# A SwiGLU block by Strassen-like products: four pairs a half in w_down's long passes, loads queued as buffers come free, three residues a half by DMA, gate's activation one half step later

## Chip, cores, metric

One Trainium2 chip, one of its cores. The metric is device time in microseconds (us) of the kernel on that core; lower is better. Times come from runs of the whole kernel and, for the parts, from one profiled execution.

## What is computed

One layer over 256 tokens of width 2048, all in float32:

```python
h  = x + W_out [ DiffAttn(group A heads) ; ConformerConv(group B channels) ]( RMSNorm(x) )
y  = h + SwiGLU( RMSNorm(h) )

a  = hn @ w_gate                      # hn (256, 2048), w_gate and w_up (2048, 5632)
bu = hn @ w_up
y  = h + (silu(a) * bu) @ w_down      # w_down (5632, 2048)
```

The change lies in the last three lines (the SwiGLU part). What comes before them (the projection w_in, attention, convolution, w_out) fills the first 390 us of the profile and keeps its code.

## The kernel before

**Precision.** A float32 operand is split into a part rounded to the matmul's format (`hi`) and a residue (`lo = x - hi`), and a product is made of three matmuls: hi·hi, lo·hi and hi·lo. Activations are the stationary side, weights the moving side, 128 k-rows by 512 columns at a time. Of a weight tile, ScalarE casts `hi` and VectorE subtracts for `lo`. For some chunks ("by DMA", `by_dma` in `round_chunk`) ScalarE instead writes the rounded `-raw` to `lo` (L323) and a transfer issued from POOL, GpSimd's queue, adds `raw` to it (L324); VectorE is spared.

**Units of work.** The SwiGLU part is a list of chunks that TensorE multiplies one after the other. Two kinds stand in it:

- a *chunk of two* (`g` or `u`): two k-rows of one block of 512 columns, for both halves of the tokens. 12 matmuls (`multiply_two`, L1014, L1015, L1020). A `g` chunk belongs to the first of two column blocks, a `u` chunk to the second (w_gate and w_up in a gate/up block; columns n and n + 1 of w_down in a pass).
- a *pair* (`s`): two k-rows and both column blocks at once, by seven products of sums in place of eight (a 2x2 scheme in the manner of Strassen and Winograd). 21 matmuls (`multiply_pair`, L993 to L995) into seven PSUM banks. Its weights need sums first (`wt`, L966 to L968, VectorE), then two casts (`wh`, L969 and L972, ScalarE) and two residues (`wlb`, `wlt`, L975 and L976, VectorE). Its activations need the matching sums: `make_forms` for the normalized input, `make_down_forms` for SwiGLU's product.

**Blocks and passes.** The 5632 hidden columns are 11 blocks of 512, in groups of 4, 4 and 3 (`FGROUPS`). A group's gate/up blocks come first (four pairs, four `g` and four `u` chunks each, in the order `ORDER = "sggsggsuusuu"`; block 0 goes another way); then w_down's *pass* over that group's rows, in two *halves* of two column blocks each (`down_pass`). A pass of a group of four ("long pass") has 16 k-rows: `ND = 2` pairs from its first two blocks and 6 `g` and 6 `u` chunks of two a half, in the orders `DORDERS[4]`. After the last chunk that is no `u` ("half end"), `bank_sums` adds the banks up on VectorE (L1094 to L1099), and in a gate/up block ScalarE takes gate's activation (L1105); after the last chunk, VectorE adds the two `u` banks (L1113, or L1154 in a pass) and multiplies (L1115). The product is transposed on TensorE (`ps_a`, L831) and becomes `ahi`/`alo` of the pass (L840, L842), or, for the first `ND` rows of a group's first two blocks, `raw_act` (L834), from which `make_down_forms` makes the pairs' operands in the following blocks. A pass adds its results to `hd` in DRAM by transfers from POOL (L1138, L1155).

**What sets the order.** Each engine runs its own list, and waits between the lists are by semaphores. The lists are written by one loop, `run_chunks`: at step t it rounds the chunk three ahead (`HI_AHEAD`), splits two ahead, and multiplies chunk t. Everything else (sums, activations, transposes, forms) runs in generators that are resumed once or more for each chunk; `lag(n)` lets n resumptions pass. SyncE's list of loads is one queue in that order too: a load that waits for its buffer holds back those behind it. Raw tiles have 5 buffers, pairs' raw tiles (`wb`) 2.

## Time and profile before

| | |
|---|---|
| median of 3 runs (lowest to highest) | 1048.29 us (1047.63 to 1048.34) |
| profiled execution: its time, its span | 1048.92 us, 1047.1 us |
| mean granted TensorE clock | 1.000 |
| busy: TensorE, VectorE, ScalarE, POOL | 99%, 86%, 59%, 10% of the span |
| matmuls in the trace | 4663 |
| read from and written to HBM | 204.24 MB, 9.44 MB |
| SwiGLU part | from 391 us on; long passes at 517 to 602 us and 769 to 854 us |

In the profile's rows a line reads: line, engine, operation, output<-inputs, shapes, count | busy us, mean ns | idle time of the engine just before, and what ended it. PE is TensorE's matmuls, PEld its weight loads, DVE VectorE, ACT ScalarE, POOL GpSimd (only its queue matters here). A window's row has its borders and length, then each engine's busy time with its count of instructions, the granted clock, the share of the 16 DMA engines and GB/s. Line numbers are those of the kernel before.

### The profile page before, as it was taken

The page shows a single profiled execution, that of the slowest core. Times are in us where ns is not written, and L with a number is a line of the kernel's source. Part 1 is how long each engine was busy: PE and PEld are TensorE (multiplying, and loading weights), DVE is VectorE, ACT ScalarE, POOL GpSimd, SP SyncE. Part 2 cuts the span into 40 slices and gives each one's busy share as a digit, 9 for nine tenths or more (in the row PEclk, how much of TensorE's full clock was granted, in tenths as well). Part 3 has the DMA queues.
Part 4 walks back from the last instruction along what each step waited for, and adds up shares of the span by engine and source line. Part 5 has one row for each costly group of instructions (what it writes and reads, how often), then busy time and mean ns, then how long its engine had stood idle before and what let it go on. Part 6 is the DMA issues. An engine that isn't in the chain of part 4 may idle for free.

```text
span 1047.1 us, 12933 instructions
## 1 busy us (share of the span) xinstructions
PE 1036.2 (99%) x4663; PEld 852.5 (81%) x4663; DVE 900.6 (86%) x1095; ACT 621.6 (59%) x786; POOL 100.5 (10%) x143
## 2 busy tenths in 40 slices
PE   9999999999999999999999999999999999999998
PEld 7888887877788788888888888888888888888886
DVE  7899889898765599999787898999878789989897
ACT  7544666755756565776463657666644446657442
POOL 0130122201100100000001010000000110000010
PEclk9999999999999999999999999999999999999999
DMA  9657654453546566987867789879757879798683
GB/s 335 227 182 280 212 163 167 154 181 134 177 153 226 194 223 214 268 266 236 232 210 188 217 271 273 256 217 285 248 175 241 219 208 291 222 287 267 187 265 85
DMA packets 113936, 231.30 MB, mean 221 GB/s; under 512 B 7504, under 2 KB 8656, under 8 KB 113616
## 3 DMA queue, kind: packets, MB, share of 16 engines
q1 hardware_dynamic: 104864, 203.71, 56.9%
q0 software_dynamic: 8864, 26.74, 13.4%
q8 instruction: 36, 0.59, 0.2%
q14 instruction: 28, 0.23, 0.1%
q10 hardware_dynamic: 144, 0.03, 0.0%
HBM read 204.24 MB, written 9.44 MB: 204 GB/s over the span
## 4 chain that ended last, share of the span: by engine, by line
PE 61%; DMA 2%; DVE 2%; issue 1%; ACT 0%; DVEq 0%; POOLq 0%
PE q L1020 12%; PE q L1014 12%; PE q L1015 12%; PE q L995 8%; PE q L993 7%; PE q L994 7%; DMA raw<-in_w_down_dram 1%; PE ps_a L831 1%; DMA wlo<-raw 1%; PE acc L365 1%; PE acc L359 1%; PE acc L360 1%; DVE wlo L329 1%; DVE wlt L976 0%; DVE wt L966 0%
## 5 line engine op out<-in xcount | busy, mean ns | idle before, releaser
L320 ACT CAST whi<-raw 128x1024 fp32r<-128x1024 f32 (+1 forms) x273 | 281.5, 1048 | 141.6 <-PE acc L360 58.9
L329 DVE TENSOR_TENSOR wlo<-raw,whi 128x1024 fp32r<-128x1024 f32 (+1 forms) x239 | 287.8, 1218 | 73.5 <-ACT whi L320 73.3
L972 ACT CAST wh<-wt 128x2048 fp32r<-128x2048 f32 x52 | 99.6, 1914 | 77.6 <-DVE wt L968 76.9
L976 DVE TENSOR_TENSOR wlt<-wt,wh 128x2048 fp32r<-128x2048 f32 x52 | 119.1, 2290 | 14.9 <-ACT wh L972 14.7
L359 PE MATMUL acc<-whi,xhi 128*128 128x512 f32 x320 | 126.9, 397 | 1.0 <-ACT whi L320 0.9
L360 PE MATMUL acc<-whi,xlo 128*128 128x512 f32 x320 | 125.2, 391 | 0.0
L1014 PE MATMUL q<-whi,chi 128*128 128x512 f32 x320 | 125.2, 391 | 0.0
L1015 PE MATMUL q<-whi,clo 128*128 128x512 f32 x320 | 124.5, 389 | 0.0
L993 PE MATMUL q<-wh,fhi 128*128 128x512 f32 x280 | 109.9, 393 | 0.0
L994 PE MATMUL q<-wh,flo 128*128 128x512 f32 x280 | 109.1, 390 | 0.0
L517 DVE SCALAR_TENSOR_TENSOR y<-upad,cw,y 128x256 f32<-128x256 f32 x240 | 102.2, 482 | 2.2 <-ACT y L510 2.2
L1014 PE MATMUL q<-whi,ahi 128*128 128x512 f32 x256 | 100.2, 391 | 0.0
L1015 PE MATMUL q<-whi,alo 128*128 128x512 f32 x256 | 99.6, 389 | 0.0
L975 DVE TENSOR_TENSOR wlb<-wb,wh 128x1536 fp32r<-128x1536 f32 x52 | 91.1, 1752 | 1.8 <-ACT wh L969 1.8
L365 PE MATMUL acc<-wlo,xhi 128*128 128x512 f32 x320 | 87.8, 396 | 2.0 <-DVE wlo L329 2.0
L1020 PE MATMUL q<-wlo,chi 128*128 128x512 f32 x320 | 85.7, 390 | 0.2 <-DMA wlo<-raw 0.2
L969 ACT CAST wh<-wb 128x1536 fp32r<-128x1536 f32 x52 | 76.6, 1474 | 0.0
L365 PEld LDWEIGHTS acc<-wlo,xhi 128*128 128x128 f32 x320 | 59.7, 189 | 15.3 <-DVE wlo L329 3.3
L359 PEld LDWEIGHTS acc<-whi,xhi 128*128 128x128 f32 x320 | 60.4, 189 | 14.3 <-ACT whi L320 1.9
L1020 PEld LDWEIGHTS q<-wlo,chi 128*128 128x128 f32 x320 | 59.9, 188 | 13.2 <-DMA wlo<-raw 0.8
L360 PEld LDWEIGHTS acc<-whi,xlo 128*128 128x128 f32 x320 | 60.4, 189 | 12.2
L1014 PEld LDWEIGHTS q<-whi,chi 128*128 128x128 f32 x320 | 60.1, 188 | 12.3
(230 smaller groups left out, 1739.1 us busy)
## 6 DMA issues: line engine op xcount, KB each, us to landing
raw<-in_w_in_dram SPq DMA_DIRECT2D x79, 512.0 KB, 4.6
raw<-in_w_down_dram SPq DMA_DIRECT2D x64, 512.0 KB, 7.2
raw<-in_w_gate_dram SPq DMA_DIRECT2D x48, 512.0 KB, 7.5
raw<-in_w_up_dram SPq DMA_DIRECT2D x48, 512.0 KB, 6.2
wb<-in_w_up_dram SPq DMA_DIRECT2D x40, 512.0 KB, 3.7
wb<-in_w_gate_dram SPq DMA_DIRECT2D x40, 512.0 KB, 4.9
wlo<-raw POOLq DMA_DIRECT2D x34, 512.0 KB, 7.1
raw<-in_w_out_dram SPq DMA_DIRECT2D x32, 512.0 KB, 4.2
```

The lines of the kernel that those rows point to most:

```text
L320: act.copy(c["hi"], c["raw"])
L329: dve.tensor_tensor(c["lo"], c["raw"], c["hi"].bitcast(F32), ALU.subtract)
L359: pe.matmul(ps[m], xhi[:, ms], hi[:, j, :], start=c["first"] and j == 0, stop=False)
L360: pe.matmul(ps[m], xlo[:, ms], hi[:, j, :], start=False, stop=False)
L365: pe.matmul(ps[m], xhi[:, ms], lo[:, j, :], start=False, stop=c["last"] and j == nk - 1)
L517: dve.scalar_tensor_tensor(y[:, ct, :], src, wk, y[:, ct, :], ALU.mult, ALU.add)
L976: dve.tensor_tensor(lot, c["t"], c["hi"][:, :SUMMED].bitcast(F32), ALU.subtract)
L993: pe.matmul(ps, hi, c["hi"][:, w], start=bool(first), stop=False)
L994: pe.matmul(ps, lo, c["hi"][:, w], start=False, stop=False)
L1014: pe.matmul(ps, xs[i][0][:, ms], hi[:, i, :], start=i == 0 and bool(c["first"].get(qs[m])), stop=False)
L1015: pe.matmul(ps, xs[i][1][:, ms], hi[:, i, :], start=False, stop=False)
L1020: pe.matmul(sum_bank(c, qs[m]), xs[i][0][:, ms], lo[:, i, :], start=False, stop=i == 1 and bool(c["last"].get(qs[m])))
```

## The change

Long passes get four pairs a half (`NDS = (4, 4, 2)`) in the order of the gate/up blocks, so 4 `g` and 4 `u` chunks are left; three of those eight get their residue by DMA. The activation's forms become twice as long and are spread over other buffers (`dhs`, `dls`). The last block's transposes use the same PSUM pool as the others' (`closing`). Loads are queued when, by the order of the loop, the buffer that they wait for has been split, raw tiles and pairs in the order in which their buffers come free (`load_freed`), no longer pairs by a fixed lead. Gate's activation is put one resumption later (`SILU_LAG`), and the additions to `hd` up to three (`HD_LAG`). The short last pass keeps two pairs and its orders.

```diff
@@ -86,8 +86,10 @@
 HD = N // P
-ND = 2
-DORDERS = {4: ("gguuggsguugsuu", "sgggugggusuuuu"), 3: ("gguusggsuu", "gggsgsuuuu")}
+NDS = (4, 4, 2)
+DORDERS = {4: (ORDER, ORDER), 3: ("gguusggsuu", "gggsgsuuuu")}
+HD_LAG = 3
+DOWN_BY_DMA = {4: (dict(g=(0, 1), u=(1,)),) * 2, 3: (dict(g=(), u=()),) * 2}
@@ -96,7 +98,9 @@
-PAIR_AHEAD = 6
+PAIR_BUFS = 2
+SILU_LAG = 1
@@ -386,32 +390,60 @@
         n = len(chunks)
-        i = j = p = 0
-        behind = [k for k in range(n) if chunks[k].get("kind") == "s"][NS]
+        i = j = 0
+        pairs = [k for k in range(n) if chunks[k].get("kind") == "s"]
+        raws = [k for k in range(n) if chunks[k].get("kind") != "s" and not chunks[k].get("spare_raw")]
+        loaded, split = set(), set()
+        def load(k):
+            if k not in loaded:
+                loaded.add(k)
+                if k in before:
+                    before[k]()
+                chunks[k]["load" if chunks[k].get("kind") != "s" else "fetch"](chunks[k])
+        def split_next():
+            chunks[j]["split"](chunks[j])
+            split.add(j)
+        ahead = [[k for k in which if k >= pairs[2]] for which in (raws, pairs)]
+        place = [{k: a for a, k in enumerate(which)} for which in (raws, pairs)]
+        def freed(side, t):
+            which, bufs = ((raws, RAW_BUFS), (pairs, PAIR_BUFS))[side]
+            if not ahead[side] or pairs[2] - 1 not in loaded:
+                return None
+            k = which[place[side][ahead[side][0]] - bufs]
+            return k if k in split and (t >= k or not chunks[k]["by_dma"]) else None
+        def load_freed(t):
+            while True:
+                ready = [(k, side) for side in range(2) if (k := freed(side, t)) is not None]
+                if not ready:
+                    return
+                load(ahead[min(ready)[1]].pop(0))
...
             while j < min(i, t + 1 + lo_lead):
-                chunks[j]["split"](chunks[j])
+                split_next()
                 j += 1
-            while p < min(n, t + 1 + PAIR_AHEAD):
-                if chunks[p].get("kind") == "s":
-                    if p < behind and p > t + hi_lead:
-                        break
-                    load_pair(chunks[p])
-                p += 1
+            load_freed(t)
             while i < min(n, t + 1 + hi_lead):
-                if i in before:
-                    before[i]()
-                chunks[i]["load"](chunks[i])
+                load(i)
+                for which in ahead:
+                    if i in which:
+                        which.remove(i)
                 chunks[i]["round"](chunks[i])
...
                 if hi_lead == lo_lead:
-                    chunks[j]["split"](chunks[j])
+                    split_next()
                     j += 1
             while j < min(n, t + 1 + lo_lead):
-                chunks[j]["split"](chunks[j])
+                split_next()
                 j += 1
+            load_freed(t)
             chunks[t]["multiply"](chunks[t])
@@ -819,7 +851,7 @@
     def transposed(j, aa):
-        last = j + 1 in FIRSTS
+        last = j + 1 in FIRSTS and NDS[group_of(j)[0]] < HD
         b = j - group_of(j)[1]
@@ -829,12 +861,15 @@
                     pe.transpose(pt[:, i, m * P : (m + 1) * P], aa[m][:, c : c + P], ident)
-            if b < 2 and 2 * t < ND:
-                raw_act[b] = lhs.tile([P, 2, S], F32, tag=("lhi", "llo")[b], name=f"ar{j}")
-                act.copy(raw_act[b], pt)
+            g = group_of(j)[0]
+            nd = NDS[g]
+            if b < 2 and 2 * t < nd:
+                if not b and not t:
+                    raw_act[g] = ffn["pool"].tile([P, 2, nd, S], F32, tag="draw", name="raw_act")
+                act.copy(raw_act[g][:, b, 2 * t : 2 * t + 2, :], pt)
                 yield from lag(3 if last else 6)
-                if b:
-                    start(make_down_forms(group_of(j)[0]))
+                if b and 2 * t + 2 == nd:
+                    start(make_down_forms(g))
                 continue
@@ -842,7 +877,10 @@
                 actT[j * (N // P) + 2 * t + i] = (hi[:, i, :], lo[:, i, :])
-            yield from lag(1 if last else 4)
+            yield from lag(1 if last else 3 if closing(j) else 4)
+    def closing(j):
+        return j + 1 in FIRSTS and NDS[group_of(j)[0]] == HD
@@ -857,39 +895,46 @@
-        fp = ffn["pool"]
+        nd = NDS[g]
         gap = lambda: lag(5 if FGROUPS[g] == 4 else 2)
-        a11, a21 = (raw_act[0][:, :, m * P : (m + 1) * P] for m in range(NM))
-        a12, a22 = (raw_act[1][:, :, m * P : (m + 1) * P] for m in range(NM))
-        hi = fp.tile([P, 7, ND, P], F32R, tag="dhi", name="dhi")
-        lo = fp.tile([P, 3, ND, P], F32R, tag="dlo", name="dlo")
-        fa, fb = (lhs.tile([P, 2, ND, P], F32, tag=t, name="dsums") for t in ("lhi", "llo"))
...
+        raw = raw_act.pop(g)
+        a11, a21 = (raw[:, 0, :, m * P : (m + 1) * P] for m in range(NM))
+        a12, a22 = (raw[:, 1, :, m * P : (m + 1) * P] for m in range(NM))
+        one = lambda tag, dt, name: lhs.tile([P, 4, P], dt, tag=tag, name=name)[:, :nd]
+        hi = [one("lhi", F32R, "dhi") for _ in range(4)]
+        lo = [one("llo", F32R, "dlo") for _ in range(4)]
+        f4, f5, f6, f2 = (one(t, F32, "dsums") for t in ("lhi", "lhi", "llo", "llo"))
+        act.copy(hi[0], a11)
+        dve.scalar_tensor_tensor(f4, a21, -1.0, a22, ALU.mult, ALU.subtract)
...
+        act.copy(hi[1], a12)
+        dve.scalar_tensor_tensor(f5, f4, -1.0, a11, ALU.mult, ALU.subtract)
...
+        act.activation(hi[2], a22, AF.Copy, scale=-1.0)
+        dve.tensor_tensor(f6, a11, a21, ALU.subtract)
...
+        hs = ffn["pool"].tile([P, 2, nd, P], F32R, tag="dhs", name="dhs")
+        for i, f in ((0, f4), (1, f5)):
+            act.copy(hs[:, i], f)
+        dve.tensor_tensor(f2, a12, f5, ALU.subtract)
...
+        act.copy(hi[3], f2)
...
+            dve.tensor_tensor(lo[i], a, hi[i].bitcast(F32), ALU.subtract)
...
+        dve.scalar_tensor_tensor(lo[2], a22, -1.0, hi[2].bitcast(F32), ALU.mult, ALU.subtract)
...
+        dve.tensor_tensor(lo[3], f2, hi[3].bitcast(F32), ALU.subtract)
...
+        ls = ffn["pool"].tile([P, 4, nd, P], F32R, tag="draw", name="dls")
+        act.copy(ls[:, 3], f6)
+        for i, (f, h) in enumerate(((f4, hs[:, 0]), (f5, hs[:, 1]), (f6, ls[:, 3]))):
+            dve.tensor_tensor(ls[:, i], f, h.bitcast(F32), ALU.subtract)
+            if i:
...
+        down_forms[g] = {f: (hi[i], lo[i]) for i, f in enumerate((0, 1, 3, 2))}
+        down_forms[g].update({4: (hs[:, 0], ls[:, 0]), 5: (hs[:, 1], ls[:, 1]), 6: (ls[:, 3], ls[:, 2])})
@@ -1045,7 +1090,7 @@
             if kind == "s":
-                c.update(p=what["p"], load=lambda c: None, round=round_pair, split=split_pair, multiply=multiply_pair,
+                c.update(p=what["p"], fetch=load_pair, by_dma=False, round=round_pair, split=split_pair, multiply=multiply_pair,
                          uses=[q for q, _, _ in PRODUCTS])
@@ -1072,17 +1117,18 @@
         k0 = j0 * HD
-        ks = [k for k in range(nb * HD) if k >= 2 * HD or k % HD >= ND]
-        twos = [dict(ks=(k0 + a, k0 + b), rows=slice(k0 + a, k0 + b + 1, b - a), k=None)
-                for a, b in zip(ks[::2], ks[1::2])]
+        nd = NDS[g]
+        ks = [k for k in range(nb * HD) if k >= 2 * HD or k % HD >= nd]
+        twos = [dict(ks=(k0 + a, k0 + b), rows=slice(k0 + a, k0 + b + 1, b - a), k=i)
+                for i, (a, b) in enumerate(zip(ks[::2], ks[1::2]))]
         for i, order in enumerate(DORDERS[nb]):
...
             end = {}
-            fast_block(order, [dict(p=p, rows=slice(k0 + p, k0 + p + HD + 1, HD)) for p in range(ND)], twos,
+            fast_block(order, [dict(p=p, rows=slice(k0 + p, k0 + p + HD + 1, HD)) for p in range(nd)], twos,
                        dict(g=(w_down, n * N), u=(w_down, (n + 1) * N)),
...
                        lambda sums, n=n, end=end: down_half(g, n, sums, end),
-                       lambda sums, n=n, end=end: down_whole(g, n, sums, end))
+                       lambda sums, n=n, end=end: down_whole(g, n, sums, end), DOWN_BY_DMA[nb][i])
@@ -1101,19 +1147,24 @@
         g, u = yield from bank_sums(q)
+        halfway.update(u=u)
+        yield from lag(SILU_LAG)
         for t in g:
             act.activation(t, t, AF.Silu)
-        halfway.update(g=g, u=u)
+        halfway.update(g=g)
     def block_done(j, q):
-        while "g" not in halfway:
-            yield
-        g, u = halfway.pop("g"), halfway.pop("u")
+        while "u" not in halfway:
+            yield
+        u = halfway.pop("u")
         for m, i in enumerate((Q3, QX)):
             dve.tensor_tensor(u[m], q[i], u[m], ALU.add)
+        while "g" not in halfway:
+            yield
+        g = halfway.pop("g")
         for m in range(NM):
             dve.tensor_tensor(u[m], u[m], g[m], ALU.mult)
-        yield from lag(4)
+        yield from lag(6 if closing(j) else 4)
         yield from transposed(j, u)
@@ -1132,6 +1183,9 @@
         gs, us = yield from bank_sums(q)
+        if not at_end(g, n):
+            end.update(us=us)
+            yield from lag(HD_LAG)
         for m in range(NM):
@@ -1152,13 +1206,17 @@
                 dve.tensor_tensor(us[m], q[i], us[m], ALU.add)
-                pool.dma_start(out=hd[m][:, (n + 1) * N : (n + 2) * N], in_=us[m], accum_op=ALU.add)
                 continue
...
                 sp.dma_start(out=out[m * P : (m + 1) * P, (n + 1) * N + a : (n + 1) * N + a + w], in_=hs)
+        if not at_end(g, n):
+            if FGROUPS[g] > 3:
+                yield from lag(HD_LAG)
+            for m in range(NM):
+                pool.dma_start(out=hd[m][:, (n + 1) * N : (n + 2) * N], in_=us[m], accum_op=ALU.add)
         if g == len(FGROUPS) - 1 and not at_end(g, n):
```

The lists show three places. First VectorE's, where the last block of the second group hands over to its long pass (`sum` is that block's product, `wt`, `wlb` and `wlt` a pair's, `wlo` a chunk's residue). Before:

```order
L1115 TENSOR_TENSOR sum_6655<-sum_6655,sum_6654 128x512
L1115 TENSOR_TENSOR sum_6657<-sum_6657,sum_6656 128x512
L329 TENSOR_TENSOR wlo<-raw,whi 128x1024 x3
L842 TENSOR_TENSOR alo_6740<-ps_a,ahi_6739 128x512
L966 TENSOR_TENSOR wt<-wb 128x1024
L967 TENSOR_TENSOR wt<-wb,wt 128x512
L968 TENSOR_TENSOR wt<-wt,wb 128x512
L329 TENSOR_TENSOR wlo<-raw,whi 128x1024
L842 TENSOR_TENSOR alo_6769<-ps_a,ahi_6768 128x512
L975 TENSOR_TENSOR wlb<-wb,wh 128x1536
L976 TENSOR_TENSOR wlt<-wt,wh 128x2048
```

And now:

```order
L1166 TENSOR_TENSOR sum_6694<-sum_6694,sum_6693 128x512
L1166 TENSOR_TENSOR sum_6696<-sum_6696,sum_6695 128x512
L1011 TENSOR_TENSOR wt<-wb 128x1024
L1012 TENSOR_TENSOR wt<-wb,wt 128x512
L1013 TENSOR_TENSOR wt<-wt,wb 128x512
L1020 TENSOR_TENSOR wlb<-wb,wh 128x1536
L1021 TENSOR_TENSOR wlt<-wt,wh 128x2048
L333 TENSOR_TENSOR wlo<-raw,whi 128x1024
L877 TENSOR_TENSOR alo_6793<-ps_a,ahi_6792 128x512
L333 TENSOR_TENSOR wlo<-raw,whi 128x1024
L1011 TENSOR_TENSOR wt<-wb 128x1024
```

The pass's second pair stands right behind the products where three chunks' residues stood (its first pair stands ahead of the block's sums now), and `alo` comes behind that pair.

Second ScalarE's list at the half end of the same block (`COPY sum` begins `bank_sums`, the two activations are gate's). Before:

```order
L320 CAST whi<-raw 128x1024
L1092 COPY sum_6654<-q_6400 128x512
L1105 ACTIVATE sum_6654<-sum_6654 128x512
L1105 ACTIVATE sum_6656<-sum_6656 128x512
L320 CAST whi<-raw 128x1024 x3
L840 CAST ahi_6739<-ps_a 128x512
```

And now:

```order
L1138 COPY sum_6693<-q_6414 128x512
L324 CAST whi<-raw 128x1024
L327 ACTIVATE wlo<-raw 128x1024
L1153 ACTIVATE sum_6693<-sum_6693 128x512
L1153 ACTIVATE sum_6695<-sum_6695 128x512
L1014 CAST wh<-wb 128x1536
L1017 CAST wh<-wt 128x2048
L324 CAST whi<-raw 128x1024
L875 CAST ahi_6792<-ps_a 128x512
```

The next unit's cast and negated copy have moved ahead of gate's activation, and a pair's casts stand ahead of the first transposed copy.

Third the POOL queue in the second long pass (`hd` is the result in DRAM; the first two rows of four are a half's `g` block, the others its `u` block). Before:

```order
L324 DMA wlo<-raw 128x1024 x14
L1138 DMA hd_85<-sum_6995 128x512
L1138 DMA hd_86<-sum_6997 128x512
L1155 DMA hd_85<-sum_6996 128x512
L1155 DMA hd_86<-sum_6998 128x512
L1138 DMA hd_85<-sum_7261 128x512
```

And now:

```order
L328 DMA wlo<-raw 128x1024 x19
L1192 DMA hd_85<-sum_7025 128x512
L1192 DMA hd_86<-sum_7027 128x512
L1219 DMA hd_85<-sum_7026 128x512
L1219 DMA hd_86<-sum_7028 128x512
L328 DMA wlo<-raw 128x1024
L1192 DMA hd_85<-sum_7334 128x512
```

Five more residues stand ahead of the first half's additions (three of that half, two of the second), and the second half's third one between the halves' additions.

More of the change, by code (lines that the diff above doesn't have):

```diff
@@ L868, in make_down_forms @@
-        act.copy(hi[:, 0], a11)
-        dve.scalar_tensor_tensor(fa[:, 0], a21, -1.0, a22, ALU.mult, ALU.subtract)
+        raw = raw_act.pop(g)
[4 more added lines that the diff above has]
+        lo = [one("llo", F32R, "dlo") for _ in range(4)]
@@ L870, in make_down_forms @@
+        f4, f5, f6, f2 = (one(t, F32, "dsums") for t in ("lhi", "lhi", "llo", "llo"))
+        act.copy(hi[0], a11)
+        dve.scalar_tensor_tensor(f4, a21, -1.0, a22, ALU.mult, ALU.subtract)
         yield from gap()
-        act.copy(hi[:, 1], a12)
-        dve.scalar_tensor_tensor(fa[:, 1], fa[:, 0], -1.0, a11, ALU.mult, ALU.subtract)
+        act.copy(hi[1], a12)
+        dve.scalar_tensor_tensor(f5, f4, -1.0, a11, ALU.mult, ALU.subtract)
         yield from gap()
-        act.activation(hi[:, 2], a22, AF.Copy, scale=-1.0)
@@ L885, in make_down_forms @@
         yield from gap()
-        pairs = [lhs.tile([P, 2, ND, P], F32R, tag=t, name="dlo2") for t in ("lhi", "llo")]
-        for i, f in ((0, fa), (1, fb)):
-            dve.tensor_tensor(pairs[i], f, hi[:, 3 + 2 * i : 5 + 2 * i].bitcast(F32), ALU.subtract)
-            yield from gap()
-        los = [lo[:, 0], lo[:, 1], lo[:, 2], pairs[0][:, 0], pairs[0][:, 1], pairs[1][:, 0], pairs[1][:, 1]]
-        down_forms[g] = {f: (hi[:, i], los[i]) for i, f in enumerate((0, 1, 3, 4, 5, 6, 2))}
+        dve.tensor_tensor(lo[3], f2, hi[3].bitcast(F32), ALU.subtract)
@@ new lines, in make_down_forms @@
+        yield from gap()
+        ls = ffn["pool"].tile([P, 4, nd, P], F32R, tag="draw", name="dls")
[3 more added lines that the diff above has]
+            if i:
+                yield from gap()
+        down_forms[g] = {f: (hi[i], lo[i]) for i, f in enumerate((0, 1, 3, 2))}
+        down_forms[g].update({4: (hs[:, 0], ls[:, 0]), 5: (hs[:, 1], ls[:, 1]), 6: (ls[:, 3], ls[:, 2])})
```

10 lines of the change are left out of this document (2 added, 8 removed).

## Prediction

> **What bounds the kernel now.** I read the page first, then who TensorE waited for, then the windows of one long pass, then the costs of VectorE's instructions in one cycle of four blocks and a pass, and last the timeline where a block hands over to the next. The page:
>
> ```profile
> span 1047.1 us, 12933 instructions
> PE 1036.2 (99%) x4663; PEld 852.5 (81%) x4663; DVE 900.6 (86%) x1095; ACT 621.6 (59%) x786; POOL 100.5 (10%) x143
> ```
>
> TensorE is busy in 99% of the span. A busy share can hide a slow pace, so the second view is who TensorE's matmuls (PE) and weight loads (PEld) waited for in the SwiGLU part (us in total, times, longest):
>
> ```profile
> PE q L1020 <- DMA wlo<-raw: 0.2, 1, 0.2
> PE q L995 <- DVE wlt L976: 0.2, 1, 0.2
> PEld q L995 <- DVE wlt L976: 2.4, 8, 0.6
> PEld q L1020 <- DMA wlo<-raw: 0.8, 2, 0.7
> ```
>
> Almost nothing. The third view is the pace, by windows: one pair unit, eight chunks of two in a row, the whole second long pass, and the blocks around it.
>
> ```profile
> core 0: us, PE busy (x) PEld busy (x) DVE busy (x) ACT busy (x) POOL busy (x), PEclk, DMA share, GB/s
> 811.99:816.75 4.76, 4.76 (x22) 3.94 (x21) 4.76 (x7) 0.39 (x1) 2.58 (x4) 1.00 0.53 50
> 816.75:838.51 21.76, 21.76 (x97) 18.02 (x96) 15.31 (x14) 11.28 (x10) 0.92 (x2) 1.00 0.89 267
> 768.74:854.15 85.41, 85.41 (x381) 70.52 (x380) 70.91 (x68) 43.21 (x39) 5.24 (x6) 1.00 0.69 205
> 602.50:643.40 40.90, 40.90 (x181) 33.70 (x180) 38.28 (x36) 23.98 (x22) 4.36 (x5) 1.00 0.92 286
> 685.23:727.00 41.77, 41.77 (x190) 34.57 (x189) 39.01 (x41) 29.19 (x30) 3.48 (x4) 1.00 0.86 252
> 727.00:768.74 41.74, 41.74 (x189) 34.55 (x188) 34.46 (x37) 24.69 (x25) 2.58 (x3) 1.00 0.80 235
> ```
>
> 21 matmuls in 4.76 us and 96 in 21.76 are both 0.2267 us each, at a granted clock of 1.00. So there the number of matmuls sets the time, and every matmul less is 0.2267 us less, as long as its operands come in time. VectorE is next: 39.0 of 41.8 us busy in a block, 70.9 of 85.4 in the pass. Of a change that takes matmuls away and gives VectorE work, the question is whether VectorE keeps up.
>
> **TensorE's side of the change.** A pair unit does two k-rows of both column blocks in 21 matmuls; the two chunks that it replaces need 2 x 12 = 24. A half of a long pass has 2 pairs and 12 chunks now (42 + 144 = 186), then 4 pairs and 8 chunks (84 + 96 = 180). Six less in each of four halves are 24 matmuls: 24 x 0.2267 = **5.44 us**, all of it on TensorE's path. Nothing is added there: the transposes keep their number, and the bytes of weights are the same. The Trainium skill (TensorE: Matmul & The Clock Gate, Part 1) gives 215.7 ns from start to start for a warm matmul of 512 columns; by that the gain would be 24 x 0.2157 = 5.2 us; the rows here are slower and decide.
>
> **VectorE's side.** Costs in the cycle from 602.5 to 854.2 us (count | busy us, mean ns | idle before):
>
> ```profile
> L329 DVE TENSOR_TENSOR wlo<-raw,whi 128x1024 fp32r<-128x1024 f32 x42 | 50.4, 1220 | 14.5 <-ACT whi L320 14.4
> L976 DVE TENSOR_TENSOR wlt<-wt,wh 128x2048 fp32r<-128x2048 f32 x21 | 48.1, 2290 | 6.0 <-ACT wh L972 5.9
> L975 DVE TENSOR_TENSOR wlb<-wb,wh 128x1536 fp32r<-128x1536 f32 x20 | 35.0, 1752 | 1.2 <-ACT wh L969 1.2
> L966 DVE TENSOR_TENSOR wt<-wb 128x1024 f32<-128x1024 f32 x20 | 24.4, 1218 | 0.0
> L967 DVE TENSOR_TENSOR wt<-wb,wt 128x512 f32<-128x512 f32 x20 | 13.8, 692 | 0.7
> L968 DVE TENSOR_TENSOR wt<-wt,wb 128x512 f32<-128x512 f32 x20 | 13.8, 692 | 0.7
> L1098 DVE TENSOR_TENSOR sum<-q,sum 128x512 f32<-128x512 f32 x6 | 4.1, 681 | 0.0
> L842 DVE TENSOR_TENSOR alo<-ps_a,ahi 128x512 fp32r<-128x512 f32 x6 | 4.1, 684 | 0.0
> L888 DVE TENSOR_TENSOR dlo<-dsums,dhi 128x512 fp32r<-128x512 f32 x2 | 1.4, 684 | 0.0
> L882 DVE TENSOR_TENSOR dlo<-ar,dhi 128x256 fp32r<-128x256 f32 x2 | 0.8, 416 | 0.0
> L972 ACT CAST wh<-wt 128x2048 fp32r<-128x2048 f32 x20 | 38.3, 1915 | 26.8 <-DVE wt L968 26.5
> L323 ACT ACTIVATE wlo<-raw 128x1024 fp32r<-128x1024 f32 x14 | 14.8, 1056 | 0.0
> ```
>
> A pair costs VectorE 1.22 + 0.69 + 0.69 + 1.75 + 2.29 = 6.64 us; four more in a pass are 26.6. Residues of chunks on VectorE go from 24 to 16 less the 6 by DMA, so 14 less at 1.22: 17.1. Net +9.5 us a pass. The activation's forms become eleven of 512 elements at 0.684, 7.5 us, where seven of 256 at 0.417 and two of 512 made 4.3; two `alo` fall away, 1.4. Net +1.8 us in the two blocks ahead of the pass. ScalarE does four more pairs for eight fewer casts and six more `wlo` at 1.06 us; it is busy 43 of 85 us there, so I cost that at nothing.
>
> Does it fit? The pass would have 70.9 + 9.5 = 80.4 us of VectorE in 85.41 - 2.72 = 82.7. Averages don't decide that; the tightest place does. It is the second pair of a block, which VectorE begins only when the block before is summed (here the block from 685.23):
>
> ```profile
> 683.71 1.23 ACT L1105 ACTIVATE sum<-sum 128x512 f32<-128x512 f32 x2 [3.55 <-DVE sum L1098]
> 684.84 1.03 ACT L320 CAST whi<-raw 128x1024 fp32r<-128x1024 f32 x1
> 690.63 0.59 ACT L834 COPY ar<-ps_a 128x512 f32<-128x512 f32 x1 [2.42 <-PE ps_a L831]
> 693.06 2.29 DVE L976 TENSOR_TENSOR wlt<-wt,wh 128x2048 fp32r<-128x2048 f32 x1 [1.33 <-ACT wh L972]
> 696.35 0.39 PE L995 MATMUL q<-wlt,fhi 128*128 128x512 f32 x1
> 737.63 1.22 DVE L329 TENSOR_TENSOR wlo<-raw,whi 128x1024 fp32r<-128x1024 f32 x1
> 738.76 0.42 DVE L884 SCALAR_TENSOR_TENSOR dlo<-ar,dhi 128x256 fp32r<-128x256 f32 x1
> ```
>
> The pair's residue is ready at 693.06 + 2.29 = 695.35 and first used at 696.35: 1.0 us to spare, after 1.33 us of waiting for ScalarE, whose cast stood behind the copy of a transpose. (The last two rows show that VectorE starts an instruction 0.09 us before the one ahead of it ends; I take that off below.)
>
> Now the same place after the change, at the hand-over from the last block of a group to its pass; E is the end of that block's matmuls. In the block VectorE does, up to the sums of its half end: four sums and products (2.7), four pairs (26.6, the last of them the pass's first), four residues (4.9), two `alo` (1.4) and seven forms (4.8): 40.4 us by durations, some 2.5 less for the overlaps, 1.3 more for the wait above. It is through about 39 us after the block's start; the half ends two chunks ahead of E, at 41.7 - 5.4 = 36.3. The six sums (0.68 each, overlapped 4.0 in all) then end near 43, at E + 1.2, where they could end before E. The last block's four sums and products end near E + 3.7, the pass's second pair's chain (6.6, and a cast of 1.9 that it waits for in part) near E + 10.4, and it is needed at E + 11.0: after a pair of 4.76, two chunks of 5.44, a transpose of four and two matmuls. So 0.5 us are left where 1.0 are now: no stall, but thin. By the same count the pairs behind it have over 1 us; in the second half, with two sums in place of four and no transposed copy in ScalarE's way, about 2. The last block's `alo`, which the pass's third and fourth chunk use, come some 2 us early.
>
> **Residues by DMA.** Each of the 12 new ones is a cast on ScalarE, an issue on POOL and an accumulating transfer:
>
> ```profile
> L324 POOL DMA_DIRECT2D wlo<-raw x34: 847/864/938, 413.6 to 967.3; - x34
> DMA to landing us min/median/max: 5.0/7.1/10.2
> q0 software_dynamic: 8864, 26.74, 13.4%
> ```
>
> 13.4% of 1047 us for 26.74 MB makes 2.75 us of all engines for one of 0.524 MB; six a pass are 16.5. The pass had a DMA share of 0.69 x 85.4 = 58.9 us; 75.4 in 82.7 is 0.91, and the window from 602.50 shows 0.92 with TensorE at its pace. In the POOL queue two residues of the second half now stand ahead of the four additions to `hd`, and the later one behind the first half's additions, whose sums are done long before. The later activation lets ScalarE's cast and `wlo` of the next block's first chunk go ahead of it; in the fence above the cast began only at 684.84, behind an activation that had waited 3.55 us for sums, so it gets earlier by about that. I cost the queue, that lag and the new load order at nothing: between -1 (the waits above shrink) and +2 us (a load meets another).
>
> **Sum.** The profiled execution took 1048.92 us around its span of 1047.1; 1048.92 - 5.44 = 1043.5. The median of the runs shown lies 0.6 below it, at 1048.29: **1042.8 us**. A measurement of this kernel can tell about 0.2% (2.1 us) from no change, so this is faster.
>
> **Rivals.**
> 1. *Waits shrink too* (0.12). Earlier loads and casts take away part of the 3.2 us of weight-load waits in the second fence: 1041 to 1042.
> 2. *VectorE eats part* (0.12). The 0.5 us left is an estimate; where chains are late by 0.25 to 0.5 us at three places in each of the two groups, 1.5 to 3.0 of the 5.4 go: 1044.3 to 1045.8. For it speaks VectorE's 80.4 of 82.7.
> 3. *No change* (0.05). Each of the eight pairs of a pass late by 0.3 us: 2 x 8 x 0.3 = 4.8 back, 1047.6.
> 4. *Slower: VectorE and ScalarE take turns* (0.05). If each pair of a pass waits 1.33 us for its cast, as in the fence above, VectorE needs 80.4 + 8 x 1.33 = 91.0 us where the pass has 85.4 now: +5.6 a pass, 1059.5. It decides from (85.4 - 80.4) / 8 = 0.63 us a pair on. Against it: over the cycle the wait is 5.9 us for 21 pairs, 0.28 each.
> 5. *Slower: POOL's issues held up* (0.03). If a busier VectorE delayed the issue of each new residue by one instruction of 2.29 us with nothing to spare, 12 x 2.29 - 5.4 = +22 us: 1070. The 34 issues took 847 to 938 ns beside a VectorE 86% busy, so it gets little. The Trainium skill (SBUF — State Buffer, "SBUF: two separate sides") warns of such an effect: an fp32 copy on VectorE can lock GpSimd out while it writes a DMA's descriptors. The trace does not show it.
>
> That the change does not do what it says is excluded for the matmuls (the built order has 24 less).
>
> **Numbers.** The forecast itself gets 0.63: 1041.8 to 1043.9. Faster by over 0.2%: 0.63 + 0.12 + 0.12 = 0.87; within: 0.05; slower: 0.08. The range takes in rivals 1 and 2 and leaves 3 to 5 out, 0.13, with a little of the ends: 1041.0 to 1046.3.
>
> **What would show it.** After: a span 5 to 6 us shorter, each long pass 82.7 us between its first pair and the next block's, 0.2267 us a matmul in it, VectorE near 80 us there, and waits of L995's loads for `wlt` of about 2 to 3 us in all. It is wrong if a pass takes over 84 us, if those waits pass 5 us, or if TensorE waits for `wlo` by DMA or for `raw` in the passes.

## The result, and the profile after

The changed kernel takes **1042.26 us** (median of 6 runs, 1042.16 to 1042.95), the kernel before 1048.24 beside it: ratio 0.9945, 95% interval 0.9935 to 0.9955, or 6.0 us less. The prediction was 1042.8, in a range from 1041.0 to 1046.3. The profiled execution after took 1042.20 us, against 1048.92 before. Lines of the kernel after are numbered higher: L995 became L1040, L976 L1021, L329 L333, L324 L328, L1105 L1153.

The page of the kernel after, three of its lines (span, busy times, and the queue of the transfers from POOL: packets, MB, share of 16 engines):

```profile
span 1040.4 us, 13004 instructions
PE 1028.9 (99%) x4639; PEld 848.0 (82%) x4639; DVE 923.1 (89%) x1109; ACT 644.9 (62%) x804; POOL 110.7 (11%) x155
q0 software_dynamic: 10592, 33.04, 16.6%
```

TensorE has 24 matmuls less, VectorE is 22.5 us busier, and 6.3 MB more go through POOL's queue. Who TensorE waited for in the SwiGLU part, all of the answer:

```profile
PE q L1040 <- DVE wlt L1021: 0.2, 1, 0.2
PEld q L1040 <- DVE wlt L1021: 1.4, 3, 0.6
```

The eight waits of weight loads for `wlt` (2.4 us) are three (1.4), and those for `wlo` by DMA are gone. The windows: the last block ahead of the second long pass, that pass, and the first long pass:

```profile
core 0: us, PE busy (x) PEld busy (x) DVE busy (x) ACT busy (x) POOL busy (x), PEclk, DMA share, GB/s
723.36:765.10 41.74, 41.74 (x189) 34.57 (x188) 40.21 (x41) 27.96 (x27) 3.34 (x4) 1.00 0.82 233
765.10:847.70 82.60, 82.60 (x370) 68.40 (x369) 77.61 (x74) 50.53 (x43) 7.64 (x11) 1.00 0.90 262
516.50:599.05 82.55, 82.55 (x369) 68.36 (x368) 77.57 (x74) 50.52 (x43) 7.60 (x11) 1.00 0.90 263
```

TensorE has no gap in either pass, at a DMA share of 0.90. The tight place, the hand-over to the first long pass (E = 516.5, where the first pass's window begins), in the timeline:

```profile
start us, us, engine line op out<-in xcount [idle before <-releaser]
517.31 0.68 DVE L1145 TENSOR_TENSOR sum<-q,sum 128x512 f32<-128x512 f32 x1
519.10 1.28 DVE L1166 TENSOR_TENSOR sum<-sum,sum 128x512 f32<-128x512 f32 x2
524.95 2.29 DVE L1021 TENSOR_TENSOR wlt<-wt,wh 128x2048 fp32r<-128x2048 f32 x1 [0.31 <-ACT wh L1017]
527.65 0.39 PE L1040 MATMUL q<-wlt,dhs 128*128 128x512 f32 x1
```

The second pair's residue is done at 524.95 + 2.29 = 527.24 and used at 527.65: 0.4 us to spare. Last, VectorE's waits within the first long pass, and POOL's issues of residues with their landing times:

```profile
DVE wlt L1021 <- ACT wh L1017: 2.2, 7, 0.3
DVE wlo L333 <- ACT whi L324: 1.8, 1, 1.8
```

```profile
L328 POOL DMA_DIRECT2D wlo<-raw x46: 845/862/938, 413.5 to 960.8; - x46
DMA to landing us min/median/max: 5.6/7.1/9.9
```

### The profile page after: what moved, and what is told of

The parts are those of the page before. It is cut to its first block, busy times and chain, and to the rows that moved or that the text cites. A ratio compares the mean times of both kernels' runs of the same rounds, so it can differ in the third digit from the quotient of the medians.

```text
span 1040.4 us, 13004 instructions
## 1 busy us (share of the span) xinstructions
PE 1028.9 (99%) x4639; PEld 848.0 (82%) x4639; DVE 923.1 (89%) x1109; ACT 644.9 (62%) x804; POOL 110.7 (11%) x155
## 4 chain that ended last, share of the span: by engine, by line
PE 62%; DVE 2%; issue 0%; ACT 0%; DVEq 0%
PE q L1059 11%; PE q L1060 11%; PE q L1065 11%; PE q L1040 9%; PE q L1038 9%; PE q L1039 9%; PE ps_a L863 1%; PE acc L369 1%; PE acc L363 1%; PE acc L364 1%; DVE wlo L333 1%; DVE wlt L1021 0%; DVE wt L1011 0%; DVE wt L1012 0%; ACT wh L1017 0%
## 5 line engine op out<-in xcount | busy, mean ns | idle before, releaser
L324 ACT CAST whi<-raw 128x1024 fp32r<-128x1024 f32 (+1 forms) x257 | 265.5, 1048 | 117.6 <-PE acc L364 59.0
L333 DVE TENSOR_TENSOR wlo<-raw,whi 128x1024 fp32r<-128x1024 f32 (+1 forms) x211 | 254.2, 1216 | 45.9 <-ACT whi L324 45.9
L1017 ACT CAST wh<-wt 128x2048 fp32r<-128x2048 f32 x60 | 114.9, 1914 | 109.3 <-DVE wt L1013 109.2
L1021 DVE TENSOR_TENSOR wlt<-wt,wh 128x2048 fp32r<-128x2048 f32 x60 | 137.4, 2290 | 19.5 <-ACT wh L1017 19.4
L1020 DVE TENSOR_TENSOR wlb<-wb,wh 128x1536 fp32r<-128x1536 f32 x60 | 105.1, 1751 | 1.3 <-ACT wh L1014 1.3
L328 POOL DMA_DIRECT2D wlo<-raw x46 | 39.7, 864 | 507.8 <-ACT wlo L327 298.2
L1014 ACT CAST wh<-wb 128x1536 fp32r<-128x1536 f32 x60 | 88.4, 1473 | 0.0
L1065 PE MATMUL q<-wlo,chi 128*128 128x512 f32 x320 | 85.6, 389 | 0.0
L1059 PE MATMUL q<-whi,ahi 128*128 128x512 f32 x192 | 74.9, 390 | 0.0
L1060 PE MATMUL q<-whi,alo 128*128 128x512 f32 x192 | 74.7, 389 | 0.0
L1011 DVE TENSOR_TENSOR wt<-wb 128x1024 f32<-128x1024 f32 x60 | 73.1, 1218 | 0.0
L1065 PEld LDWEIGHTS q<-wlo,chi 128*128 128x128 f32 x320 | 60.1, 188 | 12.6
```

The costliest lines, as they stand in the source:

```text
L324: act.copy(c["hi"], c["raw"])
L333: dve.tensor_tensor(c["lo"], c["raw"], c["hi"].bitcast(F32), ALU.subtract)
L1017: act.copy(c["hi"][:, :SUMMED], c["t"])
L1021: dve.tensor_tensor(lot, c["t"], c["hi"][:, :SUMMED].bitcast(F32), ALU.subtract)
L1059: pe.matmul(ps, xs[i][0][:, ms], hi[:, i, :], start=i == 0 and bool(c["first"].get(qs[m])), stop=False)
L1060: pe.matmul(ps, xs[i][1][:, ms], hi[:, i, :], start=False, stop=False)
```

## Experiments

Theory A: the gain is the 24 matmuls, and every other part of the change only keeps their operands in time. Rival B: the load queue and the lags take waits away and bring most of it. Each kernel is the changed one with one edit (pairs alone: several), timed against the kernel before on the same chip, which took 1048.24 to 1048.38 us beside them. A pass lasts, below, from its first matmul to the first of the next block. In the diffs `...` stands for lines left out. Where an edit adds or takes lines, the numbers behind it shift: the change's L1040 becomes L1047 or L1012, L1021 becomes L1028 or L993, and L1065 becomes L1072 or L1037.

| kernel | median us | ratio to before, 95% |
|---|---|---|
| the change | 1042.26 | 0.9945 (0.9935 to 0.9955) |
| one long pass as before | 1045.09 | 0.9966 (0.9953 to 0.9978) |
| both long passes as before | 1048.13 | 0.9996 (0.9987 to 1.0005) |
| all residues of the passes on VectorE | 1050.85 | 1.0024 (1.0015 to 1.0034) |
| loads as before | 1050.54 | 1.0023 (1.0014 to 1.0032) |
| pairs alone | 1052.96 | 1.0051 (1.0037 to 1.0064) |
| activation at once | 1044.25 | 0.9964 (0.9952 to 0.9977) |
| additions to `hd` at once | 1043.60 | 0.9956 (0.9943 to 0.9968) |
| a residue by DMA in the short pass too | 1043.78 | 0.9957 (0.9944 to 0.9969) |
| one residue a pass back on VectorE | 1044.28 | 0.9961 (0.9948 to 0.9973) |
| second half's residues back on VectorE | 1044.23 | 0.9960 (0.9946 to 0.9974) |
| closing block's lags as the others' | 1042.45 | 0.9943 (0.9931 to 0.9956) |

### One long pass as before

```diff
-NDS = (4, 4, 2)
+NDS = (4, 2, 2)
+OLD_ORDERS = ("gguuggsguugsuu", "sgggugggusuuuu")
...
-        for i, order in enumerate(DORDERS[nb]):
+        old = nb == 4 and nd == 2
+        for i, order in enumerate(OLD_ORDERS if old else DORDERS[nb]):
...
-                       ..., DOWN_BY_DMA[nb][i])
+                       ..., dict(g=(), u=()) if old else DOWN_BY_DMA[nb][i])
```

(Left out is the placing of the shorter forms in their buffers.)

> The change, but the second long pass keeps two pairs and twelve chunks a half, its old orders of forms and no residue by DMA: 12 of the 24 matmuls are back (4621). Theory A (the gain is the matmuls, at 0.2267 us each, and about 0.6 to 1.2 us of waits outside the passes): 1042.3 + 12 x 0.2267 = 1045.0 us, between 1044.5 and 1045.4; the second pass lasts 85.3 us and the first 82.55. Rival B (the new load queue and the lags bring most of it, the pairs little): within 0.7 of the changed kernel, 1042.0 to 1043.0.

1045.09 us, 2.83 more than the change for 12 matmuls (2.72). Windows of its first and second long pass:

```profile
516.45:599.00 82.55, 82.55 (x369) 68.35 (x368) 77.56 (x74) 50.54 (x43) 7.58 (x10) 1.00 0.90 262
765.00:850.40 85.40, 85.40 (x381) 70.55 (x381) 69.81 (x67) 43.06 (x39) 5.21 (x6) 1.00 0.72 214
```

The pass with old pairs lasts 2.8 us longer, with no gap in either. This is theory A's number; B's 1042 to 1043 is ruled out.

### Both long passes as before, loads and lags as in the change

```diff
-NDS = (4, 4, 2)
+NDS = (2, 2, 2)
```

(and the lines of the experiment above).

> Load queue, lags and closing block of the change, but both long passes with two pairs a half, the old orders and no residue by DMA: all 24 matmuls are back (4633). Theory A: the kernel before less only the waits that the load queue takes away, 0.5 to 1.2 us: 1047.1 to 1047.8. Rival B: 1045 or less. If the parts around the pairs cost time that the pairs pay for: 1048.5 or more.

1048.13 us, 5.9 more than the change for 24 matmuls (5.44) and above A's 1047.1 to 1047.8: without the pairs the rest of the change brings 0.2 us, and by its interval at most 1.4. B falls. What the rest takes away stands in the traces. The weight loads' waits for `wlt` in the SwiGLU part stay (2.4 us in eight before):

```profile
PEld q L1047 <- DVE wlt L1028: 2.3, 7, 0.6
```

TensorE's one wait for a residue by DMA goes. The same matmul before and then here:

```profile
422.36 0.96 PE L1020 MATMUL q<-wlo,chi 128*128 128x512 f32 x3 [0.25 <-DMA wlo<-raw]
```

```profile
421.46 0.84 PE L1072 MATMUL q<-wlo,chi 128*128 128x512 f32 x3
```

By the starts of the same matmuls in the two traces that is 0.5 us, and no other step in the SwiGLU part is over 0.2. So the traces have the low end of A's 0.5 to 1.2 us, and the medians have 0.2; their noise allows both.

### All residues of the passes on VectorE

```diff
-DOWN_BY_DMA = {4: (dict(g=(0, 1), u=(1,)),) * 2, 3: (dict(g=(), u=()),) * 2}
+DOWN_BY_DMA = {4: (dict(g=(), u=()),) * 2, 3: (dict(g=(), u=()),) * 2}
```

> The change, but all residues in the long passes are VectorE's again (the 12 by DMA are gone; same matmuls, 4609). Theory A (VectorE has 0.4 us to spare at the hand-over to a pass and is what the DMA relieves): two residues of 1.22 us more ahead of the third and fourth pair of the first half make the tightest pair late by 2 x 1.13 - 1.1 to 2 x 1.13 - 0.4, some 1 to 2 us in each of the two passes, the second half with 2.4 us to spare loses at most 0.3: 1044.5 to 1047. Rival (VectorE has room in the pass, the DMA is not needed): 1042.0 to 1042.9.

1050.85 us, 8.6 more than the change; A had 2.2 to 4.7. The timeline at the first hand-over, and windows: first pass, 4.4 us behind that hand-over, second pass:

```profile
527.57 2.29 DVE L1021 TENSOR_TENSOR wlt<-wt,wh 128x2048 fp32r<-128x2048 f32 x1 [0.32 <-ACT wh L1017]
529.92 0.50 PE L1040 MATMUL q<-wlt,dhs 128*128 128x512 f32 x1 [1.59 <-DVE wlt L1021]
```

```profile
516.84:603.09 86.25, 84.66 (x370) 69.42 (x368) 83.12 (x79) 46.70 (x39) 3.51 (x4) 0.98 0.69 214
530.00:534.40 4.40, 4.40 (x15) 3.54 (x16) 4.37 (x5) 1.28 (x1) 0.00 (x0) 0.61 0.86 295
769.66:855.51 85.85, 83.31 (x369) 68.13 (x368) 82.73 (x78) 46.38 (x39) 3.51 (x4) 1.00 0.70 214
```

The place was right: `wlt` starts 527.57 - 524.95 = 2.6 us later than in the change, and TensorE stands still for 1.6 us. Two things were missed. Behind that pause TensorE is busy all the time and yet slow: a granted clock of 0.61 over 4.4 us, which costs 4.4 x 0.39 = 1.7 us. And VectorE, 83 of 86 us busy, does not catch up: the second pass has 2.5 us of gaps at a clock of 1.00, 0.95 of them in its second half, for which A had at most 0.3 us lost. Of the 9.8 us that this profiled execution (1051.99 us) is longer, the passes hold 3.7 and 3.3; the other 2.8 lie in the blocks around them, most of it behind the passes.

### Loads as before

```diff
+PAIR_AHEAD = 6
...
-            load_freed(t)
+            while p < min(n, t + 1 + PAIR_AHEAD):
+                if chunks[p].get("kind") == "s":
+                    if p < behind and p > t + hi_lead:
+                        break
+                    load_pair(chunks[p])
+                p += 1
...
```

> The change with the loads issued as in the kernel before (pairs up to six places ahead, raw tiles as there), all else the changed kernel's. Theory A (the load queue only takes the wait of 0.5 us at 421.7 us away): 1042.5 to 1043.0. Rival B (the pairs come in time only through the new queue): pairs of the passes late, 1044.5 to 1047, with DMA named as who TensorE or VectorE waited for.

1050.54 us, 8.3 more than the change: A, by which the queue only takes a wait of 0.5 us away, is wrong by far. Its waits in the SwiGLU part, of ScalarE for raw tiles and of TensorE for residues; the change's list has neither:

```profile
ACT whi L324 <- DMA raw<-in_w_down_dram: 19.2, 14, 3.0
ACT whi L324 <- DMA raw<-in_w_up_dram: 8.3, 6, 2.1
PEld q L1037 <- DMA wlo<-raw: 10.6, 14, 2.1
PE q L1037 <- DMA wlo<-raw: 5.3, 8, 1.6
```

One residue followed in the timeline, first in the change, then here:

```profile
552.83 1.05 ACT L327 ACTIVATE wlo<-raw 128x1024 fp32r<-128x1024 f32 x1
```

```profile
558.05 1.06 ACT L327 ACTIVATE wlo<-raw 128x1024 fp32r<-128x1024 f32 x1
569.52 1.20 PE L1037 MATMUL q<-wlo,ahi 128*128 128x512 f32 x4 [1.56 <-DMA wlo<-raw]
```

The passes begin at 518.36 and 516.50, so 1.9 us of the 5.2 are an offset: the residue's first step runs 3.4 us later in the pass, and its transfer is not there in time. So the new queue is what brings the residues by DMA in time. Why the old one is late shows in what SyncE's loads waited for from 517 to 602 us (L1001 and L973 load pairs, L319 raw tiles), all of the answers, in the change and then here:

```profile
SPq L1001 <- DVE wlb L1020: 26.4, 8, 4.5
SPq L319 <- DMA wlo<-raw: 21.5, 4, 9.9
SPq L319 <- DVE wlo L333: 20.9, 10, 6.8
```

```profile
SPq L973 <- DVE wlb L992: 66.4, 8, 12.3
```

With the old order only the pairs' loads wait, 66.4 us, and no raw tile's load waits for its own buffer: that buffer was already free while the load stood behind a pair's in the list.

### Pairs alone

```diff
-HD_LAG = 3
-DOWN_BY_DMA = {4: (dict(g=(0, 1), u=(1,)),) * 2, 3: (dict(g=(), u=()),) * 2}
-SILU_LAG = 1
+HD_LAG = 0
+DOWN_BY_DMA = {4: (dict(g=(), u=()),) * 2, 3: (dict(g=(), u=()),) * 2}
+SILU_LAG = 0
```

(and the loads as in the experiment above; the closing block's lags stay).

> The four pairs a half (4609 matmuls, new orders of forms, closing lags) with the loads of the kernel before, all residues of the long passes on VectorE, and the activation and the additions to hd at their old places. The runs so far: VectorE's residues cost 8.6 us of the changed kernel, the old loads 8.3. Theory A1 (two separate causes, of which the second is mainly late residues by DMA, which fall away here): 1050 to 1053, pairs alone slower than the kernel before by 2 to 5 us. Theory A2 (they add): 1057 to 1061. Rival (only the DMA residues need the new loads, and the lags do harm with VectorE late): 1047 to 1049.5.

1052.96 us, 4.7 slower than the kernel before, within A1: the two losses do not add up, since without residues by DMA in the passes none can be late there (TensorE waits 1.6 us for such residues, all in the blocks, where it waited 5.3 with the old loads alone). Its waits for `wlt`, and a window:

```profile
PEld q L1012 <- DVE wlt L993: 8.3, 8, 2.0
PE q L1012 <- DVE wlt L993: 5.0, 6, 1.6
```

```profile
530.00:534.40 4.40, 4.20 (x13) 3.35 (x14) 4.37 (x6) 1.57 (x2) 0.00 (x0) 0.61 0.99 336
```

Again VectorE's pair at the hand-over, and again the clock at 0.61 behind it. Pairs without the rest of the change turn 6.0 us of gain into 4.7 us of loss.

### Activation at once, additions to `hd` at once

```diff
-SILU_LAG = 1
+SILU_LAG = 0
```

> The change with the activation of the gate's sums queued at once, as before, not a half step later. Theory A (ScalarE's queue then holds the cast of the next chunk behind the sums, some 3 us; the wait of 0.5 us for a residue by DMA at 421.7 us comes back, at most once a group): 1042.5 to 1043.6. Rival 1 (the cast has room): 1042.0 to 1042.5. Rival 2 (the late cast also delays VectorE's residues at the hand-over, which the last runs showed to be sensitive): 1044 to 1046.

1044.25 us, 2.0 more: above A's range and inside rival 2's. ScalarE's timeline at a block's half end, in the change and then here:

```profile
429.61 1.05 ACT L324 CAST whi<-raw 128x1024 fp32r<-128x1024 f32 x1 [0.89 <-ACT sum L1138]
432.27 1.23 ACT L1153 ACTIVATE sum<-sum 128x512 f32<-128x512 f32 x2 [0.65 <-DVE sum L1144]
```

```profile
431.62 1.23 ACT L1153 ACTIVATE sum<-sum 128x512 f32<-128x512 f32 x2 [3.54 <-DVE sum L1144]
432.76 1.03 ACT L324 CAST whi<-raw 128x1024 fp32r<-128x1024 f32 x1
```

The activation waits 3.54 us for its sums and holds the cast back by some 3 us. Here TensorE's weight loads wait five times for a residue by DMA, where the change has no such wait:

```profile
PEld q L1065 <- DMA wlo<-raw: 2.7, 5, 0.9
```

Four of the five follow from that. The residue used at 526.70 us, for one, goes out from POOL at 521.00, where the change issues it at 515.71. The first does not: the residue used at 432.06 was issued at 421.08, as early in its block as the change's at 421.73 (the rows ahead lie 0.65 us apart too), and took 10.9 us to land where the other took 8.8. By the starts of the same matmuls in the two traces the four cost 1.3 us and the first 0.7. So the mechanism is A's, and 1.3 is the upper end of A's range; why one transfer took longer, and whether the edit is to blame, no run shows. Rival 2 has the time and not the mechanism: the loads' waits for `wlt` are 1.6 us, 1.4 in the change.

```diff
-HD_LAG = 3
+HD_LAG = 0
```

> The change with the additions to hd queued on POOL without the lag of three, so that they stand ahead of the second half's residues by DMA in POOL's queue. Theory A (a residue then waits in the queue for the half's sums): TensorE waits 1.5 to 3 us for each of one or two residues in the second half of each long pass, 1045 to 1051. Rival (those sums are done before the residue's cast, the lag changes nothing): 1042.0 to 1042.8.

1043.60 us, 1.3 more, yet under A's smallest number. The two ratios' intervals overlap, but all five of its runs (1043.24 to 1043.98) lie above all six of the change. POOL's timeline in the first long pass, in the change and then here, and the waits here:

```profile
557.24 0.86 POOL L328 DMA_DIRECT2D wlo<-raw  x1 [2.02 <-ACT wlo L327]
```

```profile
558.70 1.74 POOL L1192 DMA_DIRECT2D hd<-sum  x2 [3.25 <-DVE sum L1145]
559.79 1.54 POOL L328 DMA_DIRECT2D wlo<-raw  x1
```

```profile
PEld q L1065 <- DMA wlo<-raw: 1.6, 2, 0.9
```

POOL stands at the additions for 3.25 us; the residue that the change issues at 557.24 goes out at 559.79. It had room for most of that delay: TensorE waits once in each pass, which by the starts of the same matmuls costs 0.8 and 0.6 us.

### One residue a pass back on VectorE; the second half's back

```diff
-DOWN_BY_DMA = {4: (dict(g=(0, 1), u=(1,)),) * 2, 3: (dict(g=(), u=()),) * 2}
+DOWN_BY_DMA = {4: (dict(g=(0,), u=(1,)), dict(g=(0, 1), u=(1,))), 3: (dict(g=(), u=()),) * 2}
```

> The change with one of the three residues by DMA of each long pass's first half given back to VectorE (two of twelve in all), ahead of the second pair at the hand-over. Theory A (that pair had 0.40 us to spare; one residue takes VectorE 1.13 us from start to start): TensorE waits 0.7 to 0.8 us in each pass, 1.5 in all, and the clock is not touched by so short a pause: 1043.5 to 1044.2. Rival 1 (a pause of any length there halves the clock for some 3.4 us, as behind the pause of 1.6 us with all residues on VectorE): +4 to +5, 1046 to 1047.5. Rival 2 (the room there is larger than read): 1042.0 to 1042.8.

1044.28 us, 2.0 more. The first long pass:

```profile
516.74:600.25 83.51, 82.85 (x370) 68.27 (x368) 78.71 (x75) 50.47 (x43) 7.66 (x9) 1.00 0.86 253
```

It lasts 83.51 - 82.55 = 0.96 us longer, with a TensorE gap of 0.66, at a clock of 1.00: the 0.4 us of room are real, and a short pause there leaves the clock alone. The gap is shorter than the loss mostly because the profile counts it from a matmul's end, 0.39 us after its start, where the next one would have started after 0.23. So the time is just above A's range, which counted the gap.

```diff
-DOWN_BY_DMA = {4: (dict(g=(0, 1), u=(1,)),) * 2, 3: (dict(g=(), u=()),) * 2}
+DOWN_BY_DMA = {4: (dict(g=(0, 1), u=(1,)), dict(g=(), u=())), 3: (dict(g=(), u=()),) * 2}
```

> The change with the three residues by DMA of each long pass's second half given back to VectorE (six of twelve), the first half as in the change. Theory A (the second half's first pair behind the sums has 2.4 us to spare, two of the three residues come ahead of it, 2.3 us): 0 to 0.5 us lost, 1042.2 to 1043.2. Rival (both halves pay alike for their residues): half of the 8.6 us that all twelve cost, 1045.5 to 1047.5.

1044.23 us, 2.0 more. Windows of its first long pass and of the four blocks behind, then the same four blocks in the change:

```profile
516.60:599.15 82.55, 82.55 (x370) 68.36 (x368) 79.42 (x75) 47.52 (x40) 4.41 (x6) 1.00 0.83 242
599.15:765.99 166.84, 166.35 (x746) 137.42 (x744) 155.17 (x149) 109.51 (x102) 17.27 (x20) 1.00 0.88 249
```

```profile
599.05:765.10 166.05, 166.05 (x745) 137.50 (x744) 153.77 (x147) 109.49 (x102) 16.63 (x20) 1.00 0.88 250
```

In the pass itself A is right to the hundredth: nothing is lost. But VectorE carries the delay over the pass's end, and the next block's second pair comes late: 0.8 us here. The blocks behind the second pass take 125.8 us where the change's take 124.3: 0.8 of it at the second pair again, and 0.7 at 973 us, where TensorE waits for a residue by DMA that took 10.7 us to land (9.9 in the change). A's count stopped at the pass.

### Closing lags, and one more residue by DMA

```diff
-            yield from lag(1 if last else 3 if closing(j) else 4)
+            yield from lag(1 if last else 4)
-        yield from lag(6 if closing(j) else 4)
+        yield from lag(4)
```

> The change with the closing block's two lags (3 and 6) set to 4 as for the other blocks, which moves the first forms of the last block behind the next pair's steps. Theory A (the forms are wanted late and the copy is ready before ScalarE needs the place): at most 0.3 us, 1042.0 to 1042.7. Rival (VectorE then waits for ScalarE's cast behind a copy at the hand-over, 1.33 us at each with 0.40 to spare): 0.9 us in each of two passes, 1043.7 to 1044.5.

1042.45 us, the change's own time within its runs: that part does nothing measurable.

```diff
-DOWN_BY_DMA = {4: (dict(g=(0, 1), u=(1,)),) * 2, 3: (dict(g=(), u=()),) * 2}
+DOWN_BY_DMA = {4: (dict(g=(0, 1), u=(1,)),) * 2, 3: (dict(g=(), u=()), dict(g=(3,), u=()))}
```

> The change with one more residue by DMA, that of the chunk between the two pairs of the short last pass's second half, where TensorE waits 0.45 us for VectorE at 1020.3 us. Theory A (VectorE gets 1.2 us there and the wait goes): 0.3 to 0.5 us less than the changed kernel, 1041.7 to 1042.1. Rival (the transfer lands late, or meets the outputs' writes): 1042.5 to 1045.

1043.78 us (1042.47 to 1045.17): no gain. TensorE in the timeline, in the change and then here:

```profile
1020.88 0.50 PE L1040 MATMUL q<-wlt,dhs 128*128 128x512 f32 x1 [0.18 <-DVE wlt L1021]
```

```profile
1021.10 0.73 PE L1065 MATMUL q<-wlo,ahi 128*128 128x512 f32 x2 [0.83 <-DMA wlo<-raw]
```

The wait for VectorE is gone and a longer one for the transfer stands in its place. By the starts of the same matmuls that place loses 0.7 us. The profiled execution loses 0.9 more at 972 us, ahead of the edit: the same residue that came late with the second half's back, issued as early as in the change (960.74 and 960.76), took 11.1 us to land where the change's took 9.9. In the change it lands 0.4 us ahead of its use, so this is a second place without room, and what is lost there is not shown to be the edit's. No version here beats the change.

## Why the prediction was right, step by step

- **TensorE's 24 matmuls, 5.44 us.** Right. A long pass went from 85.4 to 82.55 us, predicted 82.7; the experiment with 12 of them back cost 2.83 us, and that with all 24 back 5.9 of the 6.0 measured. By the Trainium skill's 215.7 ns (TensorE: Matmul & The Clock Gate, Part 1) an estimate would be 5.2 us; the passes agree with the rows' 0.2267.
- **VectorE's 80.4 us in the pass.** Mis-sized: 77.6. Work had moved over the window's border: the block ahead is 40.21 us busy where 34.46 were, because VectorE makes the pass's first pair there. The total, 9.5 + 1.8 = 11.3 us a group, was right: VectorE is 22.5 us busier for two groups. The step that bore the forecast, that block and the hand-over, was right: six sums predicted to end at E + 1.2, measured 517.31 + 0.68 - 516.5 = 1.5; the products at E + 3.7, measured 3.9; the second pair ready at E + 10.4, measured 10.7; needed at E + 11.0, measured 11.15. Of 0.5 us to spare (the prediction's own 11.0 - 10.4 is 0.6) 0.4 were there, and one residue more made TensorE wait.
- **Residues by DMA, queue, lag, load order at nothing.** Right for the whole change: TensorE waits for no residue by DMA, and the pass's DMA share is 0.90 (0.91 predicted). But "nothing" holds only for all of them together. Each has a price if it is missing: 8.6 us without the DMA, 8.3 without the load queue, 2.0 without the activation's lag (1.3 of it traced to the lag), 1.3 without that of the additions. The prediction named the DMA's cover and gave no price for its loss, and spoke of the load queue as something that could at best take waits away. Here it was right about the whole without knowing what the parts carry.
- **The sum.** 5.44 of the 6.0 us. The other 0.5 is as much as the one wait for a residue by DMA that goes without the pairs too, so rival 1 (0.12) is partly true by the traces; the medians, with 0.2 us for that kernel, don't settle it. The loads' waits for `wlt` are 1.4 us where 2 to 3 were predicted; these shrink only with the pairs, since with both passes as before they are 2.3. The span is 6.7 us shorter where 5 to 6 were predicted, but that compares single executions, and the one before lay 0.7 above its runs' median.
- **Rival 2 and 3, VectorE eats the gain.** Not in the change; with one residue a pass back on it, 2.0 us are eaten.
- **Rival 4, turns of VectorE and ScalarE.** It needed 0.63 us a pair; VectorE waits at most 0.3 for a pair's cast in the first long pass.
- **Rival 5, POOL's issues held up.** 46 issues took 845 to 938 ns beside a VectorE 89% busy, as 34 did before. The lock that the Trainium skill describes for fp32 copies on VectorE (SBUF — State Buffer, "SBUF: two separate sides") does not show; in the SwiGLU part VectorE runs sums, differences and products of two operands and no copy, so these runs do not put it to the test.

## What to carry to other kernels

Where one engine is busy in 99% of the span at an even pace, count what is taken off it, and spend the rest of the work on the one place where the next engine has least room; follow that engine's delay past the end of the stage, into the next block. A part that brings nothing by itself may be what the gain rests on: here the same pairs are worth -6.0 us with their loads and residues arranged, and +4.7 without. So price each such part by its absence.

## What the runs showed of the hardware

The granted clock can fall after a pause of 1.6 us. TensorE stood still that long at the first hand-over in the kernel with all residues on VectorE, and its clock was 0.61 over the 4.4 us behind (0.50 in each window of 1 us from 531 to 534); the same in the kernel with pairs alone. It does not always happen. At the second hand-over of the first of these kernels the pause was as long, and the window of that pass, above, shows a clock of 1.00:

```profile
782.73 0.50 PE L1040 MATMUL q<-wlt,dhs 128*128 128x512 f32 x1 [1.59 <-DVE wlt L1021]
```

In the kernel with the old loads a pause of 1.56 us ends at 569.52 us (above), and its window there shows the full clock:

```profile
566.00:575.00 9.00, 7.39 (x32) 5.48 (x31) 7.20 (x7) 4.64 (x4) 1.21 (x2) 1.00 1.07 234
```

Pauses of about 0.7 us left the clock at 1.00 too. The Trainium skill (TensorE: Matmul & The Clock Gate, Part 1) says that the clock is halved after an idle window of about 3.4 us, and that the window runs freely; a pause of half that length was enough here, in two of six pauses of 1.5 to 1.6 us. What decides, perhaps where the pause falls in the window, no run shows. So a stall of 1.6 us may cost 3.3 (1.6 and the 1.7 behind it).
